# Two changes to the order of VectorE's work in a fused two-layer decoder: paired softmax blocks, and dense steps issued behind the dots

## Chip, core and metric

The kernel runs on one core of a Trainium2 chip. The metric is the device time of one launch in microseconds (us), the lower the better. TensorE is called PE here, VectorE DVE, ScalarE ACT, GpSimd POOL and SyncE SP, as in the profile. Each engine takes its instructions in the order in which they stand in the built program.

## What is computed

Two decoder layers over 512 tokens of width 1024, in float32. Cut to what matters:

```python
for l in range(2):
    m   = x @ w_in[l]                                   # q, k, v, two LRU branches, two gates
    ya  = diff_attention(q, k, v)                       # 8 heads, two causal ALiBi softmax maps each:
                                                        #   (softmax(q1 k1) - lam * softmax(q2 k2)) @ v
    yr  = rg_lru(conv4(xr)) * gelu(gr)
    x   = layer_norm(ALPHA * x + (sig(ga) * (ya @ wa) + sig(gb) * (yr @ wb)) @ w_out)
    # PEER: per token 8 heads x 16 experts of 16384, chosen by two top-16s and a top-16 of their sums
    e, g = route(x)                                     # 128 expert numbers and weights per token
    x   = layer_norm(ALPHA * x + sum_j g[j] * gelu(x . u[e[j]]) * v[e[j]])
```

## The kernel before

The tokens are four blocks of 128 rows (one token per partition). `experts(l, b)` serves one block: for each of its 128 expert places j, POOL gathers one row of 2048 floats (u and v) per token with an indirect DMA (L819, 1 MB in all) into one of 8 buffers `uvt`. DVE then takes the **dot** of u with x (L822), ACT applies gelu (L829), DVE makes the weight `w` (L784), and v is added up in one of two ways: on DVE into `acc` (L790), or by ACT making a diagonal `dg` (L794) and PE two matmuls into `pv` (L796). A buffer is free for a new gather when this is done. Four blocks in two layers make 1024 places, numbered 0 to 1023 below; "dot 450" is the dot of place 450.

Everything else is called **dense**. `mixer` (attention, LRU, merges, output product) handles two blocks at a time and streams its weights as 512 KB pieces through 5 buffers `w` (L253, L275 are its matmuls). `route` (matmuls L656, L663) scores the keys; on DVE `top16` (L716 to L721) and `choose` (L728 to L767) turn the scores into the expert numbers `e` (L761) and weights `g`. `route_late` runs `choose` for the second block of a pair. "Routing" below means L716 to L767.

In the softmax of the attention, `softmax(h, i, b, po, st)` takes one head and one of the two blocks through: scores on PE into the PSUM tile `s2` (one buffer, L386), bias and row maximum on DVE (L390 to L396), two Exp on ACT (L398), a combination on DVE (L402 to L407), transposes on PE through `pt` (one buffer, L412) and the product with v into `po` (L417). The tile `pr` has two buffers; `choose` uses the same two for its one-hot tables `oh` (L753 to L758).

Two things set the order. First `run` records three streams, `gathers()`, `dense()` and `late()`, each with a clock, always going on with the one whose clock is lowest. The clock of `gathers` counts places; `PLAN` gives the dense stages their stretch of places (mixer of layer 0, blocks 2 and 3: places 30 to 222; its routing 222 to 270; its late choice 270 to 370; the same for layer 1: 270 to 470, 470 to 526, 526 to 620, and 526 to 730, 730 to 786, 786 to 880). Within a stage the yielded numbers are shares of its stretch. Second, the framework's scheduler orders the recorded instructions of each engine anew: by recorded place, but an instruction that is ready sooner by the scheduler's own estimate may be put ahead. The class `Load` counts, in recorded order, which of DVE and PE has less to do, and so chooses between L790 and L796.

Of the kernel before, what the change touches and what calls it, by code (L numbers as in the profile page):

```python
# [18 lines left out]
ALU = mybir.AluOpType  # L19
# [3 lines left out]
D = 1024  # L23
# [97 lines left out]
class Decoder:  # L121
# [227 lines left out]
    def attention(self, l, cst, blocks, x, ya, on):  # L349


        nc, t2 = self.nc, self.t2
# [25 lines left out]
        def softmax(h, i, b, po, st):  # L378
# [15 lines left out]
            nm, sm = st[:, i, 0:2], st[:, i, 2:4]  # L394
            nc.vector.tensor_reduce(nm, pr[:, :, :nk], AX.X, ALU.max)
            nc.vector.tensor_scalar(nm, nm, -0.125, None, ALU.mult)  # L396
            for m in range(2):
                nc.scalar.activation(pr[:, m, :nk], pr[:, m, :nk], AF.Exp,  # L398
                                     bias=nm[:, m : m + 1], scale=0.125,
                                     accum_out=sm[:, m : m + 1])  # L400
            yield 2.0
            nc.vector.reciprocal(st[:, i, 4:6], sm)  # L402

            nc.vector.scalar_tensor_tensor(out=st[:, i, 6:7], in0=st[:, i, 5:6],
# [42 lines left out]
        def heads(h):  # L447
            po = self.ps_t.tile([P, 512], F32, name="po", tag="po")
            st = t2.tile([P, 4, 8], F32, name="at_st", tag="at_st")
            for i, b in enumerate(blocks):  # L450
                yield from softmax(h, i, b, po, st)
            nc.scalar.copy(on[:, h, :n], po[:, :n])

        yield from project(0)
# [319 lines left out]
    def experts(self, l, b, G=2):  # L774
# [28 lines left out]
        for j0 in range(0, P, G):  # L803
# [12 lines left out]
            for i in range(G):  # L816
                j = j0 + i
                t = self.gp.tile([P, 2 * D], F32, name="uvt", tag="uv")
                nc.gpsimd.indirect_dma_start(  # L819
                    out=t, out_offset=None, in_=self.uv,  # L820
                    in_offset=bass.IndirectOffsetOnAxis(ap=e[:, j : j + 1], axis=0))
                nc.vector.scalar_tensor_tensor(out=t[:, :D], in0=t[:, :D], scalar=1.0, in1=x,  # L822
                                               op0=ALU.mult, op1=ALU.mult,
                                               accum_out=dots[:, i : i + 1])
                uvs.append(t)
                if i == 0:
                    next(prev, None)
                else:
                    nc.scalar.activation(q, dots, AF.Gelu_apprx_tanh)  # L829
                yield 1  # L830
# [10 lines left out]
    def run(self):  # L841
        nc = self.nc
        self.setup()
        self.cst = [None] * DEPTH
        self.done = set()
        self.load = Load(nc)

        def gathers():
# [35 lines left out]
        while any(live):  # L884
            free = [i for i in range(3) if live[i] and (wants[i] is None or wants[i] in self.done)]
            i = min(free, key=lambda i: (at[i], -i))
            wants[i] = None
            c = next(streams[i], None)
            if c is None:
                live[i] = False  # L890
            elif isinstance(c, tuple):
# [39 lines left out]
```

## Time and profile before

| | |
|---|---|
| median of 3 runs (lowest, highest) | 3445.73 us (3443.23, 3445.84) |
| the profiled execution: its own time | 3443.5 us |
| its span, first to last instruction | 3441.3 us |
| first dot, last gather's landing | about 306 us, about 3422 us |
| busy: PE, DVE, ACT, POOL | 2962.3, 2660.9, 1242.6, 1307.3 us |
| moved by DMA | 1290.5 MB, of which 1073.8 MB by the gathers' queue |
| chain that ended last | PE 44%, DVE 24%, DMA 19% |

A window of the trace gives each engine's busy time in a stretch, the clock granted to PE (1.00 is full), the mean busy share of the 16 DMA engines (it can read a little over 1) and the GB/s that they moved. The windows below are cut at the start of every 32nd dot, so that each holds 32 places. Records of consecutive short instructions overlap; busy time counts the overlap once. A PE matmul of float32 has two records.

### The profile page before, as it was taken

How to read it: one execution, taken by the hardware profiler on the slowest of the kernel's cores; microseconds unless marked ns; L12 is line 12 of the kernel's file. 1: busy time of each engine (PE TensorE's matmuls, PEld its weight loads, DVE VectorE, ACT ScalarE, POOL GpSimd, SP SyncE). 2: the span in 40 equal slices, each digit the busy share in tenths (PEclk: the TensorE clock that was granted, in tenths of full speed). 3: DMA queues.
4: the chain of work that ended last, by engine and by line, in shares of the span. 5: the costliest groups of instructions: out<-in, count | busy, mean ns of one | idle time of the engine just before them, and what ended most of it. 6: DMA issues, size and time to landing. Idle time of an engine off the chain costs nothing.

```text
span 3441.3 us, 38208 instructions
## 1 busy us (share of the span) xinstructions
PE 2962.3 (86%) x11832; PEld 1899.5 (55%) x11832; DVE 2660.9 (77%) x6622; ACT 1242.6 (36%) x2851; POOL 1307.3 (38%) x1033
## 2 busy tenths in 40 slices
PE   8997999999997899999996799999998687656655
PEld 8896666777763466677763366666755232212111
DVE  7765989887689577867699569777679965777776
ACT  7852356652122364633122236644122221111111
POOL 0001334444333434434333433433433344565553
PEclk9998999999999999999997999999999799877677
DMA  5455899999999999999998999999999899999997
GB/s 202 155 174 204 332 408 397 414 418 418 418 398 354 380 392 401 393 417 412 418 389 342 412 393 391 401 413 419 418 412 353 312 405 421 421 422 410 421 422 317
DMA packets 219114, 1290.54 MB, mean 375 GB/s; under 512 B 24593, under 2 KB 37137, under 8 KB 87841
## 3 DMA queue, kind: packets, MB, share of 16 engines
q0 software_dynamic: 147456, 1073.81, 77.0%
q1 hardware_dynamic: 71456, 214.30, 16.4%
q8 instruction: 96, 1.57, 0.2%
q14 instruction: 106, 0.86, 0.1%
HBM read 1285.92 MB, written 2.10 MB: 374 GB/s over the span
## 4 chain that ended last, share of the span: by engine, by line
PE 44%; DVE 24%; DMA 19%; issue 6%; POOL 3%; ACT 3%; POOLq 0%; SPq 0%; DVEq 0%; ACTq 0%
DMA uvt<-uv_dram,e 19%; PE ps_mm L253 18%; PE pv L796 16%; DVE uvt L822 8%; POOL uvt L819 3%; DVE acc L790 3%; PE ps_mm L275 3%; PE ps_ln L313 1%; PE ps_qk L253 1%; DVE oh L756 1%; DVE ef L758 1%; PE s L386 1%; DVE oh L753 1%; PE ps_mm L656 1%; PE po L417 1%
## 5 line engine op out<-in xcount | busy, mean ns | idle before, releaser
L819 POOL DMA_INDIRECT uvt<-uv_dram,e x1024 | 1304.7, 1274 | 2101.5 <-PE pv L796 655.1
L796 PE MATMUL pv<-uvt,dg 128*128 128x512 f32 x2712 | 1417.4, 662 | 379.3 <-ACT dg L794 377.8
L822 DVE SCALAR_TENSOR_TENSOR uvt<-uvt,xn 128x1024 f32<-128x1024 f32 x1024 | 1243.8, 1220 | 248.3 <-DMA uvt<-uv_dram,e 244.4
L796 PEld LDWEIGHTS pv<-uvt,dg 128*128 128x128 f32 x2712 | 527.8, 206 | 1094.7 <-ACT dg L794 604.4
L253 PE MATMUL ps_mm<-room_xT,w 128*128 128x256 f32 x2304 | 538.6, 380 | 0.7 <-ACT room_xT L285 0.7
L829 ACT ACTIVATE q<-dots 128x2 f32<-128x2 f32 x512 | 104.1, 203 | 1132.3 <-DVE uvt L822 1117.4
L253 PEld LDWEIGHTS ps_mm<-room_xT,w 128*128 128x128 f32 x2304 | 430.4, 190 | 108.8 <-issue 53.9
L790 DVE SCALAR_TENSOR_TENSOR acc<-uvt,w,acc 128x1024 f32<-128x1024 f32 x346 | 443.6, 1282 | 7.9
L794 ACT ACTIVATE dg<-ident,w 128x128 f32<-128x128 f32 x678 | 257.4, 398 | 290.3 <-DVE w L784 171.1
L784 DVE TENSOR_TENSOR w<-q,g 128x2 f32<-128x2 f32 x512 | 80.7, 158 | 208.9 <-ACT q L829 203.9
L656 PE MATMUL ps_mm<-room_xT,w 128*128 128x256 f32 (+1 forms) x1056 | 241.5, 377 | 0.0
L656 PEld LDWEIGHTS ps_mm<-room_xT,w 128*128 128x128 f32 x1056 | 194.7, 194 | 42.7 <-issue 19.9
L829 ACT ACT_TABLE_LOAD x115 | 147.5, 1283 | 19.6 <-DVE uvt L822 17.0
L238 DVE TENSOR_TENSOR wsp<-raw,wsp 128x1024 fp32r<-128x1024 f32 x80 | 97.1, 1222 | 27.0 <-ACT wsp L237 24.8
L275 PEld LDWEIGHTS ps_mm<-w,room_xT 128*128 128x128 f32 x768 | 90.8, 192 | 8.5 <-issue 7.1
L275 PEld LDWEIGHTS ps_mm<-w,room_m 128*128 128x128 f32 x768 | 89.2, 192 | 9.2 <-issue 8.4
L275 PE MATMUL ps_mm<-w,room_xT 128*128 128x128 f32 x768 | 92.6, 275 | 0.0
L253 PE MATMUL ps_mm<-room_yr,w 128*128 128x256 f32 x384 | 90.1, 380 | 0.0
L253 PE MATMUL ps_mm<-room_ya,w 128*128 128x256 f32 x384 | 89.5, 379 | 0.0
L275 PE MATMUL ps_mm<-w,room_m 128*128 128x128 f32 x768 | 89.3, 275 | 0.0
L237 ACT CAST wsp<-raw 128x1024 fp32r<-128x1024 f32 x80 | 82.7, 1052 | 14.8 <-PE ps_mm L253 7.8
L822 DVE DVE_READ_ACCUMULATOR uvt<-uvt,xn 128x1 f32 x1024 | 84.1, 82 | 0.0
(196 smaller groups left out, 2980.7 us busy)
## 6 DMA issues: line engine op xcount, KB each, us to landing
w<-wpk_dram SPq DMA_DIRECT2D x304, 512.0 KB
raw<-wpk_dram SPq DMA_DIRECT2D x80, 512.0 KB
uvt<-uv_dram,e POOLq DMA_INDIRECT x1024
gw<-gpk_dram SPq DMA_DIRECT2D x32, 128.0 KB
sk<-spk_dram SPq DMA_DIRECT2D x64, 64.0 KB
xn<-x_dram SPq DMA_DIRECT2D x4, 512.0 KB
out_dram<-xn SPq DMA_DIRECT2D x8, 256.0 KB
lq<-lqk_dram SPq DMA_DIRECT2D x2, 128.0 KB
```

Source lines behind the costliest of these rows:

```text
L237: self.nc.scalar.copy(hi, raw)
L238: self.nc.vector.tensor_tensor(lo, raw, hi.bitcast(F32), ALU.subtract)
L253: self.nc.tensor.matmul(ps[:, :n], w, x, start=i == 0, stop=i == len(steps) - 1)
L275: self.nc.tensor.matmul(out[:, i], x(slice(i * P, (i + 1) * P)), w, start=j == 0, stop=j == len(steps) - 1)
L656: nc.tensor.matmul(pq[:, :n], w[:, kc, :], self.acts_x.plain[:, kc, t0 : t0 + n], start=kc == 0, stop=kc == KC - 1)
L784: nc.vector.tensor_tensor(w, q, g[:, j0 : j0 + G], ALU.mult)
L790: nc.vector.scalar_tensor_tensor(out=acc, in0=t[:, D:], scalar=w[:, i : i + 1], in1=acc, op0=ALU.mult, op1=ALU.add)
L794: nc.scalar.activation(dg, self.ident, AF.Copy, scale=w[:, i : i + 1])
L796: nc.tensor.matmul(pv[:, half], dg, t[:, D + half * 512 : D + (half + 1) * 512], start=not began[0], stop=j == P - 2)
L819: nc.gpsimd.indirect_dma_start(out=t, out_offset=None, in_=self.uv, in_offset=bass.IndirectOffsetOnAxis(ap=e[:, j : j + 1], axis=0))
L822: nc.vector.scalar_tensor_tensor(out=t[:, :D], in0=t[:, :D], scalar=1.0, in1=x, op0=ALU.mult, op1=ALU.mult, accum_out=dots[:, i : i + 1])
L829: nc.scalar.activation(q, dots, AF.Gelu_apprx_tanh)
```

## The change

Three edits. In `softmax` the step that ended after the Exp is cut in two, with a yield after the row maximum. `heads` takes both blocks of a head through `softmax` in step (`zip`) where it took one block after the other. And each dot is remembered in `self.dot`; whatever `dense()` and `late()` then record on DVE gets an order edge to the last recorded dot: it has to stand behind it in DVE's queue, with no wait for it to finish.

```diff
@@ softmax
             nc.vector.tensor_scalar(nm, nm, -0.125, None, ALU.mult)
+            yield 1.0
             for m in range(2):
                 nc.scalar.activation(pr[:, m, :nk], pr[:, m, :nk], AF.Exp,
                                      bias=nm[:, m : m + 1], scale=0.125,
                                      accum_out=sm[:, m : m + 1])
-            yield 2.0
+            yield 1.0
@@ heads
-            for i, b in enumerate(blocks):
-                yield from softmax(h, i, b, po, st)
+
+            for costs in zip(*(softmax(h, i, b, po, st) for i, b in enumerate(blocks))):
+                yield sum(costs)
@@ experts
-                nc.vector.scalar_tensor_tensor(out=t[:, :D], in0=t[:, :D], scalar=1.0, in1=x,
-                                               op0=ALU.mult, op1=ALU.mult,
-                                               accum_out=dots[:, i : i + 1])
+                self.dot = nc.vector.scalar_tensor_tensor(
+                    out=t[:, :D], in0=t[:, :D], scalar=1.0, in1=x, op0=ALU.mult, op1=ALU.mult,
+                    accum_out=dots[:, i : i + 1]).ins
@@ run
-            c = next(streams[i], None)
+            if i and self.dot is not None:
+
+                with self.tc.issue_after(self.dot):
+                    c = next(streams[i], None)
+            else:
+                c = next(streams[i], None)
```

After the edits line numbers from 397 on are one higher, from the end of `heads` on two higher (L824 is the dot, L786 `w`, L792 `acc`, L798 `pv`).

What the built programs hold: 4960 DVE instructions before and 4957 after, 2645 and 2620 on ACT (300 and 272 of them table loads), 346 and 343 times L790. Counted between dots in DVE's order, the routing instructions:

| places | 192-223 | 224-255 | 256-287 | 416-447 | 448-479 | 480-511 | 512-543 | 672-703 | 704-735 | 736-767 | 768-799 | 800-863 |
|---|---|---|---|---|---|---|---|---|---|---|---|---|
| before | 153 | 171 | 31 | 73 | 226 | 25 | 32 | 55 | 222 | 155 | 0 | 0 |
| after | 0 | 217 | 105 | 0 | 30 | 190 | 102 | 0 | 20 | 190 | 114 | 108 |

The accumulations L790 stand where they stood: 14, 3, 2, 16, 13, 0, 3, 16, 13, 2, 1 in these windows (the last apart). Of the dense DVE instructions recorded between dots 448 and 511 the mean one stood 41 dots ahead of its recorded place before, between dots 64 and 127 0.6 dots ahead, between dots 0 and 63 2.1 dots behind; now none stands ahead.

DVE, layer 1's routing of blocks 0 and 1. Each L822 or L824 row is a dot; the first row of both pieces is dot 455. Before:

```order
L822 SCALAR_TENSOR_TENSOR uvt_12912,dots_12910<-uvt_12912,xn1_4375 128x1024
L790 SCALAR_TENSOR_TENSOR acc_11704<-uvt_12865,w_12915,acc_11704 128x1024
L758 TENSOR_REDUCE ef_13550<-oh_13562 128x16
L822 SCALAR_TENSOR_TENSOR uvt_12922,dots_12910<-uvt_12922,xn1_4375 128x1024
L756 TENSOR_TENSOR oh_13581<-oh_13581,ca_13532 128x864
L784 TENSOR_TENSOR w_12931<-q_12911,g3_115 128x2
L716 MAX sv_13611<-sc_13635 128x8
L790 SCALAR_TENSOR_TENSOR acc_11704<-uvt_12922,w_12931,acc_11704 128x1024
L822 SCALAR_TENSOR_TENSOR uvt_12928,dots_12926<-uvt_12928,xn1_4375 128x1024
L758 TENSOR_REDUCE ef_13550<-oh_13581 128x16
L718 MAX_INDEX si_13612<-sv_13611,sc_13635 128x8
L761 CAST e0_108<-ef_13550 128x32
```

Now, from dot 455 on:

```order
L824 SCALAR_TENSOR_TENSOR uvt_12918,dots_12916<-uvt_12918,xn1_4375 128x1024
L824 SCALAR_TENSOR_TENSOR uvt_12928,dots_12916<-uvt_12928,xn1_4375 128x1024
L786 TENSOR_TENSOR w_12937<-q_12917,g3_115 128x2
L792 SCALAR_TENSOR_TENSOR acc_11712<-uvt_12928,w_12937,acc_11712 128x1024
L824 SCALAR_TENSOR_TENSOR uvt_12934,dots_12932<-uvt_12934,xn1_4375 128x1024
L824 SCALAR_TENSOR_TENSOR uvt_12944,dots_12932<-uvt_12944,xn1_4375 128x1024
L786 TENSOR_TENSOR w_12953<-q_12933,g3_115 128x2
L792 SCALAR_TENSOR_TENSOR acc_11712<-uvt_12944,w_12953,acc_11712 128x1024
```

The routing (L716, L718, L753 to L761) has left this place. DVE thirty dots on, from dot 487, before:

```order
L822 SCALAR_TENSOR_TENSOR uvt_13372,dots_13370<-uvt_13372,xn1_4375 128x1024
L822 SCALAR_TENSOR_TENSOR uvt_13400,dots_13370<-uvt_13400,xn1_4375 128x1024
L784 TENSOR_TENSOR w_13434<-q_13371,g3_115 128x2
L822 SCALAR_TENSOR_TENSOR uvt_13431,dots_13429<-uvt_13431,xn1_4375 128x1024
L822 SCALAR_TENSOR_TENSOR uvt_13444,dots_13429<-uvt_13444,xn1_4375 128x1024
L784 TENSOR_TENSOR w_13475<-q_13430,g3_115 128x2
```

Now, from dot 487:

```order
L824 SCALAR_TENSOR_TENSOR uvt_13378,dots_13376<-uvt_13378,xn1_4375 128x1024
L718 MAX sv_13318<-sc_13353 128x8 x2
L720 MAX_INDEX si_13319<-sv_13318,sc_13353 128x8 x2
L723 MATCH_REPLACE sc_13353<-sv_13318,sc_13353 128x128 x2
L718 MAX sv_13318<-sc_13353 128x8 x2
L720 MAX_INDEX si_13319<-sv_13318,sc_13353 128x8 x2
L824 SCALAR_TENSOR_TENSOR uvt_13406,dots_13376<-uvt_13406,xn1_4375 128x1024
L718 MAX top0_12897<-sc_13355 128x8 x2
```

Here it stands now, in the stretch that `PLAN` gives it. PE, one head of the second mixer (places 32 to 64), before:

```order
L386 MATMUL s2_5027<-kT0_104,qT_4802 128x256
L386 MATMUL s2_5027<-kT1_4376,qT_4802 128x128
L386 MATMUL s2_5027<-kT0_104,qT_4802 128x256
L386 MATMUL s2_5027<-kT1_4376,qT_4802 128x128
L253 MATMUL ps_mm_5042<-room_xT_4378,w_5043 128x256 x8
L796 MATMUL pv_3552<-uvt_5009,dg_5062 128x512 x2
L489 MATMUL pg_5075<-xc_5068,gw_4986 128x256
L386 MATMUL s2_5183<-kT0_104,qT_4802 128x256
L386 MATMUL s2_5183<-kT1_4376,qT_4802 128x256
L489 MATMUL pg_5078<-xc_5068,gw_4986 128x256
L253 MATMUL ps_mm_5094<-room_xT_4378,w_5095 128x256
L412 MATMUL pt_5088<-ident_88,pr_5032 128x128 x3
```

Now:

```order
L386 MATMUL s2_5027<-kT0_104,qT_4803 128x256
L386 MATMUL s2_5027<-kT1_4376,qT_4803 128x128
L386 MATMUL s2_5027<-kT0_104,qT_4803 128x256
L386 MATMUL s2_5027<-kT1_4376,qT_4803 128x128
L253 MATMUL ps_mm_5049<-room_xT_4378,w_5050 128x256 x4
L386 MATMUL s2_5036<-kT0_104,qT_4803 128x256
L386 MATMUL s2_5036<-kT1_4376,qT_4803 128x256
L386 MATMUL s2_5036<-kT0_104,qT_4803 128x256
L386 MATMUL s2_5036<-kT1_4376,qT_4803 128x256
L253 MATMUL ps_mm_5049<-room_xT_4378,w_5050 128x256 x4
```

The scores of the head's second block follow four projection matmuls behind the first block's; its first transposes (L413, not in the piece) stand 30 matmuls behind them.

## Rows read from the trace of the kernel before

**Rows 1.** Page, 40 equal slices of 86 us: DMA share in tenths, GB/s

```profile
DMA  5455899999999999999998999999999899999997
GB/s 202 155 174 204 332 408 397 414 418 418 418 398 354 380 392 401 393 417 412 418 389 342 412 393 391 401 413 419 418 412 353 312 405 421 421 422 410 421 422 317
```

**Rows 2.** Windows: stretch, length, busy us (records) of PE PEld DVE ACT POOL, PEclk, DMA, GB/s

```profile
436.00:537.60 101.60, 99.23 (x409) 67.04 (x410) 90.18 (x249) 56.14 (x119) 41.47 (x32) 1.00 0.99 394
736.90:840.90 104.00, 102.31 (x453) 76.27 (x452) 85.70 (x161) 38.39 (x82) 46.88 (x33) 1.00 1.02 418
950.00:1058.60 108.60, 97.03 (x376) 65.02 (x376) 97.48 (x332) 27.48 (x84) 42.93 (x32) 0.97 1.00 399
1058.60:1152.80 94.20, 70.60 (x162) 32.03 (x163) 83.47 (x307) 25.43 (x66) 38.49 (x32) 0.91 0.90 341
1152.80:1256.90 104.10, 99.39 (x347) 60.07 (x346) 63.35 (x163) 45.13 (x97) 36.66 (x32) 0.95 0.99 397
1665.10:1776.60 111.50, 102.06 (x500) 73.35 (x499) 88.67 (x263) 24.40 (x71) 38.98 (x32) 0.95 1.00 408
1776.60:1885.00 108.40, 77.52 (x229) 42.23 (x227) 108.40 (x416) 26.69 (x70) 42.07 (x32) 0.86 0.92 354
1885.00:1962.90 77.90, 61.65 (x130) 24.90 (x131) 45.89 (x89) 15.08 (x49) 32.30 (x32) 0.96 0.99 402
1962.90:2067.00 104.10, 99.05 (x358) 60.67 (x356) 68.39 (x164) 43.13 (x96) 36.71 (x32) 0.95 0.99 393
2471.00:2579.80 108.80, 100.56 (x480) 69.29 (x479) 82.57 (x236) 21.26 (x60) 39.31 (x33) 0.94 1.01 414
2579.80:2688.20 108.40, 84.99 (x282) 50.34 (x281) 108.37 (x404) 26.59 (x77) 40.85 (x32) 0.89 0.92 347
2688.20:2780.50 92.30, 63.74 (x121) 25.23 (x120) 84.89 (x258) 28.30 (x61) 38.44 (x32) 0.87 0.88 330
2943.00:3022.50 79.50, 47.30 (x77) 16.01 (x76) 57.60 (x95) 10.66 (x35) 45.34 (x32) 0.82 1.01 421
```

**Rows 3.** Waits in 1776.6 to 1885.0: who waited for whom, us, times, longest

```profile
POOL uvt L819 <- PE pv L796: 18.7, 7, 6.6
POOL uvt L819 <- DVE acc L790: 11.3, 3, 7.5
POOL uvt L819 <- DVE top L716: 9.6, 4, 4.3
```

**Rows 4.** DVE groups, 1776.6 to 1885.0: line, op, shapes, count | busy, mean ns | idle before

```profile
L822 DVE SCALAR_TENSOR_TENSOR uvt<-uvt,xn 128x1024 f32<-128x1024 f32 x33 | 39.9, 1210 | 0.0
L790 DVE SCALAR_TENSOR_TENSOR acc<-uvt,w,acc 128x1024 f32<-128x1024 f32 x13 | 16.5, 1272 | 0.0
L784 DVE TENSOR_TENSOR w<-q,g 128x2 f32<-128x2 f32 x16 | 2.4, 148 | 0.0
```

**Rows 5.** DMA issues on the page: size of one weight piece

```profile
w<-wpk_dram SPq DMA_DIRECT2D x304, 512.0 KB
```

**Rows 6.** POOL groups, in 1776.6 to 1885.0, then in 2862.0 to 3022.5

```profile
L819 POOL DMA_INDIRECT uvt<-uv_dram,e x32 | 42.1, 1315 | 68.8 <-PE pv L796 18.7 <-DVE acc L790 11.3 <-DVE top L716 9.6
...
L819 POOL DMA_INDIRECT uvt<-uv_dram,e x64 | 83.2, 1299 | 76.7 <-PE pv L796 47.6 <-DVE acc L790 17.2 <-issue 5.9
```

**Rows 7.** ACT groups of the whole span: the table loads ahead of gelu and Exp

```profile
L829 ACT ACT_TABLE_LOAD x115 | 147.5, 1283 | 19.6 <-DVE uvt L822 17.0 <-DVE at_st L402 0.6
...
L398 ACT ACT_TABLE_LOAD x64 | 82.1, 1283 | 1.1
```

**Rows 8.** DVE's waits over the whole span

```profile
DVE uvt L822 <- DMA uvt<-uv_dram,e: 244.4, 244, 3.2
...
DVE at_st L402 <- ACT pr L398: 16.5, 23, 2.5
...
DVE oh L753 <- PE po L417: 1.0, 3, 0.6
```

**Rows 9.** Window before the first gather, columns as in group 2

```profile
0.00:260.00 260.00, 243.62 (x1929) 231.88 (x1930) 183.94 (x420) 191.96 (x364) 2.57 (x9) 1.00 0.52 177
```

More of the change, by code (lines that the diff above doesn't have):

```diff
@@ L845, in run @@
         self.done = set()
+        self.dot = None
         self.load = Load(nc)
```

## Prediction, made before the changed kernel was run

> **What bounds the kernel now.** I read the page's slices first. From the fifth slice on the DMA share is at 8 to 9 tenths and the rate mostly between 390 and 422 GB/s, but it falls to 354 and 380, 389 and 342, 353 and 312 [rows 1]: three dips, one per routing after the first. So the gathers and the weights fill the DMA engines, and what can be won is in the dips. Then I cut the trace at every 32nd dot, because the change is about where work stands between dots. An undisturbed window without weights takes 79.5 us at 421 GB/s; a mixer window with its weights takes 104.0 us at 418, with PE busy for 102.3 of it [rows 2]. Both run as fast as the DMA engines go. In the dips DVE is full: 108.40 us of 108.40 in places 448 to 479, 108.37 of 108.40 in 704 to 735, 84.89 of 92.30 in 736 to 767, 97.48 of 108.60 in 192 to 223, while PE sinks to 64 to 85 us and its granted clock to 0.86 to 0.91 [rows 2]. POOL shows how this reaches the DMA: it waits to issue the next gather for `acc` and even for a MAX8 of the routing, which are no producers of its buffer but the instructions behind which the releasing one had queued on DVE [rows 3]. The cause is in the order, not in the amount of work: DVE's queue holds the routing some 40 dots ahead of its recorded place, packed into one window (226 routing instructions in places 448 to 479, 25 in the next one), while `Load` had given that window 13 accumulations on DVE as if the routing were not there. The window behind it then has too little for DVE: 45.89 us of 77.90 [rows 2].
>
> **What a dip costs.** At 418 GB/s the bytes of a window would take (rate/418) of its time. The excess by [rows 2], in order of place: dip one (192 to 255) 4.9 + 17.4 = 22.3 us; dip two (416 to 511) 2.7 + 16.6 + 3.0 = 22.3; dip three (672 to 767) 1.0 + 18.4 + 19.4 = 38.8. In all 83.4 us. That is the pool from which the tie can draw.
>
> **The tie (issue behind the dots).** It adds no instruction and no semaphore; it moves the routing back to the stretch that `PLAN` gives it. Price of the routing per instruction: in 1776.6 to 1885.0, 108.4 us busy, less 32 dots of 1.210 (38.7), 13 accumulations (16.5) and `w` (2.4) [rows 4], leaves 50.8 us for 226 instructions, 0.225 us each. In 2688.2 to 2780.5, 84.9 less 38.7, 2.4 and two accumulations of 1.272 leaves 41.3 for 155, 0.266 each (more of them one-hot passes). With the counts of the order after, DVE has to do:
>
> - places 224 to 255: 38.7 + 2.4 + 3 x 1.272 + 217 x 0.225 to 0.266 = 94 to 103 us;
> - 480 to 511: 41.1 + 190 x the same = 84 to 92 us;
> - 736 to 767: 41.1 + 2 x 1.272 + 190 x the same = 86 to 94 us;
> - the windows that the routing leaves (192, 448 and 704 on): under 75 us, since at most 30 routing instructions stay.
>
> DMA needs 79.5 us for 32 gathers plus 1.25 us for each weight piece of 512 KB at 418 GB/s [rows 2, 5]. The score matmuls in PE's order after (79, 50 and 73, eight to a piece) put 9.9, 6.2 and 9.1 pieces into the first three: 91.9, 87.3 and 90.9 us. So DVE and DMA are about level there: DVE is over by 2 to 11 us in the first, by -3 to 5 and -5 to 3 in the others. Nowhere is there a second window like 448 to 479, where DVE's 108.4 us stood against 91.8 us of bytes (108.4 x 354/418).
>
> What stays: a window in which all three engines are this busy has not run at 418 in the trace but at 393 to 397 (places 256 to 287 and 512 to 543), a loss of 5.2 and 6.2 us [rows 2]. I take 8 us for the first heavy window (it is also over by some 6 at mid-range), 5 and 6 for the other two, 3 for each of the three that were emptied, and 2 for place 768 on, which now gets 114 routing instructions but has only 79.5 us of gathers to meet: 8 + 5 + 6 + 9 + 2 = 30 us. The tie gains 83.4 - 30 = **53 us**. Bounds: 83 if nothing stays, 23 if twice as much stays.
>
> Nothing waits in exchange by the order: the expert numbers of the block that starts at place 256 stand behind dot 234 (was 211), those for 512 behind 484 (448), for 768 behind 744 (708). With 8 buffers POOL wants them 8 places early, so 14, 20 and 16 places are left, at 2.5 us a place 35 us or more. What is late next is DMA itself.
>
> **The paired softmax.** No operation is added. Table loads fall from 300 to 272: 28 x 1.283 us [rows 7] = 36 us of ACT. ACT is busy for 56 of 101.6 us in an attention window [rows 2], and DVE's waits on Exp add up to 16.5 us in the whole span [rows 8]: I take 0, with 16 as the most to be won. In the first 260 us, which the tie doesn't reach, PE is busy for 243.6 [rows 9]; with some 11 us of that idle time at the start, 5 us is the most to be won. To be lost: the pair holds both `pr` buffers at once and the late choice's one-hot tables want the same two. DVE waits for one of them 1.0 us in all, 3 times [rows 8]. Taking 0.3 us for each of the 48 one-hot chains of the three late choices that fall beside a mixer gives 16 us; I take 0, as DVE and PE have other work queued there.
>
> **Sum.** 3443.5 us (the profiled execution's own time: the span of 3441.3 and 2.2 around it) - 53 = 3390.5. The median of the runs, 3445.73, is 2.2 us above that execution, so I say **3392 us**, 1.6% less.
>
> **Rivals.** (a) *Slower: dots block the dense steps.* DVE takes its queue in order, and dots wait for gathers: 244 times, 1.0 us in the mean [rows 8]. A softmax step behind a waiting dot passes that on to PE, whose transposes and products stand in one queue with `pv`, and `pv` frees the gathers' buffers. The 24 heads of the three mixers beside gathers have 4 steps each: 96 waits of 1.0 us would be 96 us, 3443.5 - 53 + 96 = 3486. It decides from 0.55 us a step. Against it: in places 0 to 127 the old order already has the dense steps about where they were recorded (2.1 dots behind and 0.6 ahead in the mean of its halves), and PE is busy for 99.2 of 101.6 us in places 32 to 63, at 394 GB/s [rows 2]. The Trainium skill ("Perfetto Trace Analysis", Per-instruction lifecycle) says that PE can pull weight loads ahead while "ACT/DVE/GPSIMD are strict FIFO": by that rule nothing on DVE can pass a waiting dot, which is this rival; no row here shows an instruction passing another.
>
> (b) *No change: POOL was held by the port, not by the buffers.* If DVE's running instructions themselves lengthened POOL's gather issue, the same DVE work later would cost the same: 3443.5. Then an issue should take longer in a dip than in a calm stretch; it takes 1315 ns against 1299 [rows 6]. The Trainium skill ("SBUF — State Buffer", Two separate sides) has such a rule: VectorE and GpSimd share a port pair, and descriptors made on GpSimd starve while VectorE holds it. The rows give it 0.016 us x 32, half a us per dip.
>
> (c) *Less: the heavy windows become the new dips.* If DVE's waits on PE and ACT inside the score chain make each heavy window 10 us longer than taken (PE's own routing matmuls now stand among the dots there), the gain is 53 - 30 = 23: 3420.
>
> (d) *More: the paired softmax also lifts the attention stretches to 418 GB/s.* Six slices of the page run at 391 to 401 there (392, 401, 393 and 393, 391, 401) [rows 1] and lose 28 us by the same reckoning: 3443.5 - 83 - 28 = 3332.
>
> That the tie does nothing is excluded by the counts of the order.
>
> **How the numbers follow.** Chances: the forecast (30 to 80 us gained) 0.60, (c) 0.16, (d) 0.08, (b) or a balance of gains and losses 0.05, (a) 0.11. A measurement of this kernel can tell about 0.2%, 7 us, from no change. Faster is 0.60 + 0.16 + 0.08 = 0.84, same 0.05, slower 0.11. The range goes from 3350 (the tie's bound of 83 with some of the softmax's) to 3432, through (c) as far as a gain of 12 us; it leaves out (d), (a) and (b), with the far ends some 0.2.
>
> **What would show it.** Right: no window of 32 dots with DVE busy over 98% of it; the dips at places 448 and 704 gone, those windows at 90 to 96 us and over 400 GB/s; places 480 to 511 longer than 77.9 us (about 92); PE's clock over 0.9 in all of them; DMA share 0.97 or more from 436 us on. Wrong: DVE idle before dots while PE waits on DVE in the mixers (a); POOL waiting on the routing's L761 behind dots 234, 484 or 744; or the three heavy windows over 105 us (c).

## The result, and the profile after

The changed kernel takes 3409.28 us (median of 4 runs, 3407.21 to 3417.96) against 3445.78 for the kernel before (3443.23 to 3446.22): a ratio of 0.990, 95% interval 0.9882 to 0.9919. That is 36.5 us less. The forecast was 3392 us, 53 us less, with a range of 3350 to 3432. Sign and range hold; the gain is two thirds of the one forecast.

The profiled execution took 3407.21 us, its span 3405.4. First the page, with the lines that answer to [rows 1] and [rows 7]: busy time by engine, then DMA share and GB/s in 40 slices of 85 us, the shares of the chain that ended last, and the table loads ahead of gelu.

```profile
PE 2953.0 (87%) x11844; PEld 1904.5 (56%) x11844; DVE 2654.6 (78%) x6619; ACT 1208.6 (35%) x2826; POOL 1331.9 (39%) x1033
...
DMA  5455899999999999999999999999999989999997
GB/s 193 165 173 200 311 409 411 396 418 418 419 408 404 356 411 390 416 418 403 418 408 412 387 408 395 391 393 413 416 418 411 385 353 422 421 422 414 422 422 311
...
PE 50%; DMA 21%; DVE 16%; ACT 6%; issue 5%; POOL 3%; SPq 0%; POOLq 0%; DVEq 0%; ACTq 0%
...
L831 ACT ACT_TABLE_LOAD x99 | 127.0, 1283 | 10.0 <-DVE uvt L824 5.1
```

The dips are narrower: 354 and 380, 389 and 342, 353 and 312 GB/s [rows 1] have become 356, 387 and 385 with 353. No engine's amount of work has moved much: DVE was busy for 2660.9 us and is for 2654.6. On the chain DVE went from 24% to 16% and PE from 44% to 50%.

Now the windows of 32 places, as in [rows 2] (columns: stretch, length, busy us and records of PE, PEld, DVE, ACT, POOL, PEclk, DMA share, GB/s). Of the kernel after, in order: places 192, 224, 256, 448, 480, 512, 704, 736 and 768 on.

```profile
945.30:1041.30 96.00, 79.55 (x312) 48.75 (x311) 64.84 (x123) 20.79 (x60) 41.53 (x32) 0.89 1.00 410
1041.30:1145.00 103.70, 94.56 (x316) 57.15 (x314) 96.35 (x391) 25.82 (x81) 38.61 (x32) 0.96 1.00 397
1145.00:1241.40 96.40, 86.54 (x278) 49.88 (x279) 83.05 (x291) 47.28 (x100) 34.82 (x31) 0.95 0.93 373
...
1749.10:1842.80 93.70, 80.62 (x264) 47.33 (x262) 68.99 (x174) 18.48 (x63) 41.00 (x32) 0.90 1.00 408
1842.80:1938.90 96.10, 88.88 (x291) 51.72 (x292) 85.59 (x320) 30.34 (x86) 37.46 (x31) 1.00 1.00 401
1938.90:2031.40 92.50, 86.39 (x278) 49.23 (x277) 80.16 (x250) 41.65 (x87) 39.26 (x33) 0.94 0.97 392
...
2545.10:2638.90 93.80, 75.62 (x216) 39.48 (x215) 66.79 (x142) 21.62 (x63) 41.54 (x31) 0.80 1.01 412
2638.90:2738.50 99.60, 93.45 (x325) 57.22 (x323) 89.78 (x357) 26.68 (x83) 36.15 (x32) 1.00 0.96 383
2738.50:2826.00 87.50, 66.83 (x135) 26.14 (x134) 72.98 (x237) 24.35 (x60) 41.65 (x34) 0.90 0.92 364
```

Places 448 and 704 on, DVE's full windows of 108.4 us, now take 93.7 and 93.8 at 408 and 412 GB/s. In exchange 224 on went from 94.2 to 103.7 and 480 on from 77.9 to 96.1.

One reckoning makes windows comparable, the prediction's own: what a window loses is its length times (1 - rate/418). All losses together account for the change of the span to within 1 us in the change and the tie alone (5 us in the pairing alone), since the bytes are the same. By group, in us (dips: places 192 to 287, 416 to 543, 672 to 799; mixers: the other places from 32 to 671; the first 32 places apart; the span is that of the profiled execution):

| | first 32 | dips | mixers | rest | span |
|---|---|---|---|---|---|
| before | 21.1 | 94.9 | 29.6 | -1.9 | 3441.3 |
| after | 25.3 | 50.3 | 35.1 | -2.5 | 3405.4 |
| tie alone | 22.6 | 55.6 | 20.7 | -0.3 | 3396.7 |
| pairing alone | 24.1 | 102.8 | 43.1 | -2.5 | 3469.7 |

So the change wins 44.6 us in the dips and loses 5.5 in the mixers and 4.2 in the first stretch: 35 of the span's 35.9 us. Each row is one execution. The change with four weight buffers for five, a kernel of the same time (below), reads 22.9, 46.4, 36.5 and -1.9, so a difference of some 4 us in one group says little.

### The profile page after: what moved, and what is told of

Same layout as the page of the kernel before. It is cut to its first block, busy times and chain, and to the rows that moved or that the text cites. A ratio compares the mean times of both kernels' runs of the same rounds, so it can differ in the third digit from the quotient of the medians.

```text
span 3405.4 us, 38230 instructions
## 1 busy us (share of the span) xinstructions
PE 2953.0 (87%) x11844; PEld 1904.5 (56%) x11844; DVE 2654.6 (78%) x6619; ACT 1208.6 (35%) x2826; POOL 1331.9 (39%) x1033
## 4 chain that ended last, share of the span: by engine, by line
PE 50%; DMA 21%; DVE 16%; ACT 6%; issue 5%; POOL 3%; SPq 0%; POOLq 0%; DVEq 0%; ACTq 0%
DMA uvt<-uv_dram,e 21%; PE pv L798 19%; PE ps_mm L253 16%; DVE uvt L824 5%; PE ps_mm L658 5%; PE ps_mm L275 4%; POOL uvt L821 3%; DVE acc L792 2%; PE ps_ln L313 1%; PE ps_sc L665 1%; PE s L386 1%; DVE oh L755 1%; DVE ef L760 1%; PE po L418 1%; PE ps_qk L253 1%
## 5 line engine op out<-in xcount | busy, mean ns | idle before, releaser
L821 POOL DMA_INDIRECT uvt<-uv_dram,e x1024 | 1329.3, 1298 | 2041.4 <-PE pv L798 778.9
L798 PE MATMUL pv<-uvt,dg 128*128 128x512 f32 x2724 | 1411.2, 655 | 321.4 <-ACT dg L796 320.2
L824 DVE SCALAR_TENSOR_TENSOR uvt<-uvt,xn 128x1024 f32<-128x1024 f32 x1024 | 1243.7, 1220 | 266.4 <-DMA uvt<-uv_dram,e 260.6
L798 PEld LDWEIGHTS pv<-uvt,dg 128*128 128x128 f32 x2724 | 530.4, 205 | 986.0 <-ACT dg L796 506.4
L253 PEld LDWEIGHTS ps_mm<-room_xT,w 128*128 128x128 f32 x2304 | 438.5, 192 | 121.2 <-issue 54.2
L792 DVE SCALAR_TENSOR_TENSOR acc<-uvt,w,acc 128x1024 f32<-128x1024 f32 x343 | 440.3, 1284 | 10.6 <-ACT acc L813 0.2
L786 DVE TENSOR_TENSOR w<-q,g 128x2 f32<-128x2 f32 x512 | 80.6, 157 | 245.1 <-ACT q L831 235.9
L658 PEld LDWEIGHTS ps_mm<-room_xT,w 128*128 128x128 f32 x1056 | 196.1, 195 | 44.2 <-issue 21.9
L275 PEld LDWEIGHTS ps_mm<-w,room_m 128*128 128x128 f32 x768 | 92.6, 197 | 19.1 <-issue 10.4
L534 ACT ACTIVATE mth<-ps_mm 128x256 f32<-128x256 f32 x64 | 24.5, 383 | 201.3 <-PE ps_mm L253 201.2
L253 PEld LDWEIGHTS ps_mm<-room_ya,w 128*128 128x128 f32 x384 | 71.4, 190 | 34.9 <-ACT mth L534 16.6
```

The source lines that it names most:

```text
L253: self.nc.tensor.matmul(ps[:, :n], w, x, start=i == 0, stop=i == len(steps) - 1)
L275: self.nc.tensor.matmul(out[:, i], x(slice(i * P, (i + 1) * P)), w, start=j == 0, stop=j == len(steps) - 1)
L658: nc.tensor.matmul(pq[:, :n], w[:, kc, :], self.acts_x.plain[:, kc, t0 : t0 + n], start=kc == 0, stop=kc == KC - 1)
L786: nc.vector.tensor_tensor(w, q, g[:, j0 : j0 + G], ALU.mult)
L792: nc.vector.scalar_tensor_tensor(out=acc, in0=t[:, D:], scalar=w[:, i : i + 1], in1=acc, op0=ALU.mult, op1=ALU.add)
L798: nc.tensor.matmul(pv[:, half], dg, t[:, D + half * 512 : D + (half + 1) * 512], start=not began[0], stop=j == P - 2)
```

## Experiments

The theory to be tested: the routing stood too dense between the dots, DVE's queue could not serve the dots in time, so the buffers came free late; the tie cures this, and the pairing is worth nothing. Against it stand a cost of the tie (dots that block dense steps), a cost of the pairing, and PE or the accumulations as the true limit of the crowded windows. Every kernel was compared with the kernel before on its own chip; that one stood at 3445.7 to 3448.3 us each time.

**The two halves apart.** The tie alone, that is the change with the pairing taken out:

```diff
-            yield 1.0
             for m in range(2):                  # the Exp
...
-            yield 1.0
+            yield 2.0
...
-            for costs in zip(*(softmax(h, i, b, po, st) for i, b in enumerate(blocks))):
-                yield sum(costs)
+            for i, b in enumerate(blocks):
+                yield from softmax(h, i, b, po, st)
```

> Only the order edge behind the dots; the softmax goes one block after the other as before. If the tie carries the whole gain (my term of 0 for the paired softmax): 3405 to 3414 us, as the changed kernel's 3409, with places 448 to 479 at 94 us or less. If the paired softmax carries a part of it: over 3418 us.

Measured: 3396.16 us (5 runs, 3391.92 to 3399.64), ratio 0.9844 (0.983 to 0.9857). That is 52 us less than before by the medians, 49 to 56 over its runs; its profiled execution, whose span of 3396.7 us the tables use, is one of its slower ones. And the pairing alone, the change with the edge to the dot left out:

> Only the paired softmax, no order edge. If it is worth nothing: 3440 to 3450 us, the three dips still there (places 448 to 479 at about 108 us with DVE full). If it is a part of the gain: 3425 to 3438 us. If it costs time, for instance through the two pr buffers that the one-hot tables want too: over 3452 us, and then the tie alone must be faster than the change.

Measured: 3471.5 us (3467.99 to 3475.07), ratio 1.0065 (1.0051 to 1.0079): 23 us slower than before. Beside the tie the pairing costs 13 us by the medians (3409.3 against 3396.2), or 16 when each kernel is taken from the kernel before on its own chip (36.5 us less against 52.1). In the pairing alone the third dip grew. These are its places 736 on, columns as above:

```profile
2706.30:2808.50 102.20, 67.61 (x124) 26.65 (x124) 100.60 (x355) 30.97 (x66) 41.50 (x31) 0.85 0.84 305
```

Against [rows 2] the window is 9.9 us longer, with DVE full and 305 GB/s. In its order 218 routing instructions stand there, 155 before: without the tie, the scheduler moves the routing when the softmax is rewritten. The table above shows the rest of the loss in the mixers (29.6 to 43.1).

**Whether the accumulations fill the dips.** The kernel before, with those of the crowded windows put on PE:

```diff
                 vector = self.load.dve + 1.22 <= self.load.pe + 1.72
+                n = (4 * l + b) * P + j
+                if 192 <= n < 256 or 448 <= n < 480 or 704 <= n < 768:
+                    vector = False
```

> The kernel before, with the routing as early as it was, but in places 192 to 255, 448 to 479 and 704 to 767 every accumulation goes to PE: 16, 13 and 14 fewer on DVE, 1.28 us each, 55 us in all. If the dips are DVE's fullness in these windows: 30 to 50 us off, 3396 to 3416 us, places 448 to 479 at 92 to 96 us. If the dips come from the routing instructions themselves holding up POOL's gathers (rival b): 3438 to 3448 us, as those stand where they stood.

Measured: 3451.18 us, ratio 1.0007 (0.9998 to 1.0016): nothing. DVE was relieved all the same, as places 448 on show; below the window stand all waits of DVE in it (who waited for whom, us, times, longest).

```profile
1785.40:1893.20 107.80, 91.36 (x282) 50.58 (x281) 96.29 (x407) 30.70 (x85) 38.31 (x32) 0.97 0.94 360
```

```profile
DVE sv L716 <- ACT sc L670: 10.4, 3, 4.7
DVE w L784 <- ACT q L832: 0.8, 3, 0.3
```

Busy time fell from 108.40 us [rows 2] to 96.29, but now DVE stands for 10.4 us before the first MAX8 of a `top16`, which waits for scores that ACT has not copied yet. 96.3 + 10.4 + 0.8 is 107.5 of 107.8 us: the queue is as full as before, with a wait in the place of the work. Both expectations failed here, and the run corrects the reading of the dips: DVE's queue is held by what waits in it as well as by its work. Why the scores come late is not settled. The routing may stand too early, or the accumulations that are now on PE may stand ahead of the score matmuls: ACT's wait for these doubled (the same places before, then in this run), and POOL's for `pv` rose from 18.7 us [rows 3] to 44.6.

```profile
ACT sc L670 <- PE ps_sc L663: 6.3, 6, 2.3
...
ACT sc L670 <- PE ps_sc L663: 12.5, 6, 3.7
```

So moving accumulations from DVE to PE does not help while the order stays; what less work in all would do was not tried.

**How dense the routing may stand.** Three kernels with the tie alone and other stretches in `PLAN`. In the first the routing gets 32, 40 and 40 places for 48, 56 and 56; in the second the mixers end 14 to 16 places earlier and it gets 62, 72 and 72:

```diff
-    (0, [2, 3], 30, 222, 270, 370),
-    (1, [0, 1], 270, 470, 526, 620),
-    (1, [2, 3], 526, 730, 786, 880),
+    (0, [2, 3], 30, 222, 254, 370),   # first     # second:    30, 208, 270, 370
+    (1, [0, 1], 270, 470, 510, 620),              #            270, 454, 526, 620
+    (1, [2, 3], 526, 730, 770, 880),              #            526, 714, 786, 880
```

> The tie alone (e1, 3396 us) with the three later routings squeezed by the plan: places 222 to 254, 470 to 510 and 730 to 770. Places 224 to 255, 480 to 511 and 736 to 767 then hold 305, 245 and 265 routing instructions in DVE's order (217, 190, 190 in e1). If the routing's density between the dots makes a dip, also with the tie: DVE needs 113 to 125, 96 to 106 and 102 to 112 us there (103.7, 96.6 and 100.0 us in e1), the windows behind them get some back, 3400 to 3425 us. If these windows are as long as they are for DMA's or PE's sake: 3390 to 3400 us.

> The tie alone with the three routings spread: places 208 to 270, 454 to 526 and 714 to 786. The same three windows hold 152, 148 and 148 routing instructions, the ones before them 70, 94 and 74. If density makes the loss: 93 to 96 us in each of the three, 3380 to 3390 us, faster than the tie alone. If the mixers, which get 14 to 16 places less, lose as much because PE is full there: 3392 to 3402 us.

Measured: 3424.07 us (ratio 0.9935, 0.9918 to 0.9951) and 3391.27 us (0.9848, 0.9831 to 0.9864). The windows from place 224 on, of the tie alone, of the squeezed and of the spread routing, with 217, 305 and 152 routing instructions in the order, one line from each kernel:

```profile
1041.20:1144.90 103.70, 94.62 (x316) 57.02 (x314) 96.30 (x390) 25.73 (x81) 38.89 (x32) 0.94 1.00 399
```

```profile
1045.90:1161.60 115.70, 98.86 (x323) 58.01 (x322) 113.56 (x505) 33.83 (x92) 34.13 (x32) 0.96 0.95 364
```

```profile
1055.00:1147.30 92.30, 84.31 (x262) 46.20 (x260) 80.02 (x308) 27.56 (x78) 37.11 (x34) 1.00 1.00 404
```

103.7, 115.7 and 92.3 us: the window's length follows the routing in it, and so it does at 480 (96.6, 103.5, 95.1) and 736 (100.1, 112.3, 89.6). A longer window also moves more bytes, so not all of it is lost. By the reckoning above the three kernels lose 4.7, 14.9 and 3.1 us at 224, 4.2, 15.6 and 3.2 at 480, 8.9, 19.1 and 4.1 at 736, and 55.6, 82.1 and 44.1 us in all dips. So squeezing the routing brings a good part of the dips back, also with the tie, and spreading it wins less than the lengths say. The window of the squeezed kernel at 224 is DVE's alone: 113.56 us busy and one wait group left, which is the whole rest of the 115.7 us:

```profile
DVE uvt L823 <- DMA uvt<-uv_dram,e: 2.1, 2, 2.0
```

The spread does not get all of this as time: its mixers have 14 to 16 places less, and places 64 to 95 went from 98.5 to 107.8 us. The third kernel keeps the mixer of layer 0 as it was and spreads the routing of layer 1 alone:

> The tie without the pairing, with the mixers of layer 1 ending 16 places earlier (454 and 714 for 470 and 730), so that each routing of layer 1 has 72 places for its 56; layer 0 keeps its stretch. If the routing's density sets the heavy windows and squeezing a mixer costs only what e6_spread showed in the windows concerned (layer 0 lost 4.3 us there, the two of layer 1 gained 1.7 and 6.3), the time is 3383 to 3391 us, less than both e1_tie_only (3396) and e6_spread (3391), with 148 routing instructions in places 480 to 511 and 736 to 767 at 89 to 95 us. If the windows' gains and losses don't add up (a gain in one is given back in the next, since the DMA engines have the same bytes to move), it is 3391 to 3397 us.

Measured: 3396.9 us (4 runs, 3389.88 to 3399.61), ratio 0.986 (0.9844 to 0.9877). Its profiled execution is the fastest of the four; there the heavy windows of layer 1 take 93.6 and 91.4 us and the span is 3388.1, as adding up the windows had it. The other three are at 3396 to 3400, like the tie alone. So the gains of single windows are not shown to add up. The spread has the lowest median of all kernels here, 3391.27 us, but by the ratios to the kernel before on the same chip (0.9844, 0.9848, 0.986) the tie alone, the spread and this one can't be told apart. All three are faster than the change, whose interval begins at 0.9882.

The opposite, a routing that ends 12 places later (222 to 282, 470 to 538, 730 to 798, the next mixers from 282 and 538 on):

> The tie alone with the three routings spread toward later places (222 to 282, 470 to 538, 730 to 798; the mixers behind begin 12 places later), so that no mixer is squeezed as in e6. 168, 148 and 158 routing instructions in the three heavy windows (217, 190, 190 in e1), 152, 152 and 140 in the ones behind them. By density: 94 to 98 us in the heavy windows, 95 to 98 behind the first two, 3383 to 3393 us. If the gain of the heavy windows is lost behind them, where the late choice and the next mixer begin: 3393 to 3402 us.

Measured: 3407.84 us, ratio 0.9883 (0.9866 to 0.9899), 12 us slower than the tie alone and outside both expectations. The heavy windows got shorter (98.2, 95.9 and 95.7 us) with 168, 148 and 158 routing instructions, but they lose no less in sum: 5.2, 6.7 and 8.0 us for 4.7, 4.2 and 8.9. More is lost in places 192 (6.2 us for 2.0), 320 (6.4 for 1.2) and 704 on (5.9 for 1.6). By the groups of the table the dips lose 64.4 us for 55.6, the mixers 20.7 as with the tie alone. A mixer that begins later may explain places 320 and 704 on, but not 192 on, where the plan is that of the tie alone. So the density of the routing is not the whole account; what this kernel loses by stays open.

**Whether PE sets the heavy windows.** PE is busy for 94.6 of 103.7 us there. The tie alone, with half of PE's expert work left out in places 224 to 255, 480 to 511 and 736 to 767 and DVE's order kept:

```diff
-                    for half in range(2):
+                    n = (4 * l + b) * P + j
+                    k = 2
+                    if j < P - 2 and (224 <= n < 256 or 480 <= n < 512 or 736 <= n < 768):
+                        k = 1
+                        self.load.pe += 0.009 + 512 / 596
+                    for half in range(k):
```

> The tie alone, with the second of the two pv matmuls left out in places 224 to 255, 480 to 511 and 736 to 767 (29, 32 and 30 places that accumulate on PE): some 26 us less on PE in each, DVE's order as in e1. If the rest of the loss in these windows (103.7, 96.6, 100.0 us in e1) is PE, on which the score matmuls and nearly all accumulations now stand: each shorter by 5 to 12 us, 3370 to 3385 us. If DVE's routing alone sets them: within 2 us of e1 in each, 3390 to 3400 us.

Measured: 3400.53 us (2 runs), ratio 0.9865 (0.9845 to 0.9884), not faster than the tie alone. Places 224 on:

```profile
1042.50:1143.60 101.10, 77.36 (x264) 48.88 (x262) 96.30 (x390) 27.72 (x85) 36.62 (x32) 0.90 1.02 412
```

PE lost 17 us of work and the window 2.6 us. DVE's 96.30 us are untouched, and so nearly is the window's length. By the reckoning it loses 1.5 us for 4.7, but the windows at 480 and 736 lose 6.1 and 7.8 for 4.2 and 8.9, so the three together lose 15.4 for 17.8. PE is not what sets them.

**Whether dots block the mixers' steps.** Rival (a) asked for a kernel in which only the routing is tied, not the mixers' DVE steps (without the pairing):

```diff
-            if i and self.dot is not None:
+            if i and self.dot is not None and (i == 2 or self.routing):
```

`self.routing` is set while `dense()` records a `route` and cleared for a `mixer`.

> The tie for the routing and the late choice alone; the mixers' DVE steps are free as before, the softmax goes one block after the other. If the gain is the routing's place: 3390 to 3402 us, as e1. If tying the mixers' steps costs time because they wait behind dots (rival a): 3375 to 3389 us. If the mixers gain by it too: over 3403 us.

Measured: 3416.45 us, ratio 0.9912 (0.9896 to 0.9929). The routing's tie gives 30 us, and the mixers' tie another 20, where rival (a) wanted a loss. By the reckoning the mixers lose 30.1 us, as before the change (29.6), where the tie alone loses 20.7; the dips lose 62.9 for 55.6, most of the difference in places 256 on (14.9 for 9.9). Why the mixers gain by being tied was not tried.

**What the pairing costs.** The two windows that grew most against the tie alone are 288 on (105.4 us for 98.8) and 576 on (107.6 for 100.1), where a late choice runs beside a mixer. Two kernels: the change with 4 weight buffers for 5, which makes room, and that one with a third buffer for `pr` and `oh`:

```diff
-        self.wp = pool("weights", 5)
+        self.wp = pool("weights", 4)          # both kernels
...
-            pr = t2.tile([P, 2, 512], F32, name="pr", tag="pr")
+            pr = t2.tile([P, 2, 512], F32, name="pr", tag="pr", bufs=3)     # the second; oh likewise
```

> The changed kernel (both edits, 3409 us) with 4 weight buffers in place of 5, which frees 4 KB per partition: the base for the next kernel. 3405 to 3440 us.

> The same with a third buffer for pr in the freed room. If the 13 us that the paired softmax costs beside the tie (3409 against 3396) come from the pair holding both pr buffers, which the late choice's one-hot tables also want: 8 to 14 us less than with 4 weight buffers and two pr, with places 288 to 351 and 576 to 607 shorter. If they come from something else (order on PE, the one s2 buffer, bigger steps on DVE): within 4 us of it.

Measured: 3409.47 us (3404.62 to 3411.16), the same as the change, and 3404.53 us (3403.9 to 3406.32), ratio 0.988. Places 576 on of the change, then of the third buffer:

```profile
2131.60:2239.20 107.60, 102.56 (x440) 69.07 (x439) 89.92 (x205) 60.63 (x127) 40.41 (x34) 0.98 0.95 381
```

```profile
2132.80:2233.90 101.10, 99.92 (x439) 67.68 (x438) 85.58 (x200) 62.40 (x129) 41.82 (x33) 1.00 1.00 402
```

With a buffer more the window is nearly as short as without the pairing. POOL's waits in the change's window (who waited for whom, us, times, longest):

```profile
POOL uvt L821 <- PE pv L798: 24.8, 11, 4.5
POOL uvt L821 <- DVE sm_st L767: 16.4, 2, 12.0
POOL uvt L821 <- DVE acc L792: 11.2, 3, 5.7
```

The longest wait of the third row, 5.7 us up to 2149.5, is for an accumulation that frees a buffer and stands behind steps of the late choice. In DVE's order of time (start, us, line, shape, idle before):

```profile
2141.95 1.06 DVE L755 TENSOR_TENSOR oh<-iota,pf 128x864 f32<-128x864 f32 x1 [0.38 <-PE po L418]
2142.93 1.22 DVE L824 SCALAR_TENSOR_TENSOR uvt<-uvt,xn 128x1024 f32<-128x1024 f32 x1
...
2144.07 1.05 DVE L758 TENSOR_TENSOR oh<-oh,ca 128x864 f32<-128x864 f32 x1
2145.04 1.05 DVE L755 TENSOR_TENSOR oh<-iota,pf 128x864 f32<-128x864 f32 x1
2146.01 1.05 DVE L760 TENSOR_REDUCE ef<-oh 128x16 f32<-128x864 f32 x1
2146.97 1.05 DVE L758 TENSOR_TENSOR oh<-oh,ca 128x864 f32<-128x864 f32 x1
2147.94 1.28 DVE L792 SCALAR_TENSOR_TENSOR acc<-uvt,w,acc 128x1024 f32<-128x1024 f32 x1
2149.13 1.05 DVE L760 TENSOR_REDUCE ef<-oh 128x16 f32<-128x864 f32 x1
2150.10 1.22 DVE L824 SCALAR_TENSOR_TENSOR uvt<-uvt,xn 128x1024 f32<-128x1024 f32 x1
```

The chain waits for `po`, since a pair holds both `pr` buffers until its product with v; then two one-hot chains come at once and stand 6 us between two dots. The 12.0 us of the second row are another wait, up to 2210.5: two such chains stand there as well, from 2194.7 to 2200.7, but behind them also steps of the mixer, so the chains are only a part of it. With the third buffer POOL has no wait on L767 in this window.

The third buffer shortens the two windows by 14 us and the time by some 5 only, between its two expectations; the intervals of the two kernels (0.9875 to 0.9908 and 0.9863 to 0.9896) overlap. The rates tell a part of why. At 288 the change already ran at 409 GB/s; the shorter window has 397, so it moves fewer bytes and wins nothing. At 576 the rate rose from 381 to 402, a loss of 9.5 us that became 3.9. By the groups of the table the mixers now lose 25.0 us, for 36.5 with four weight buffers and 35.1 in the change, near the 20.7 of the tie alone: what the pairing loses in the mixers goes for the most part with the shared buffers. But the dips lose 52.9 us for 46.4 (50.3 in the change), 5.6 of it in places 704 on, where both others lose 1.3. Why the dips take a part back was not tried and stays open.

**Whether the routing should also stand behind `w` and `acc`.** The change, with the dense steps tied to the last dot, `w` or accumulation, whichever was recorded last:

```diff
-            nc.vector.tensor_tensor(w, q, g[:, j0 : j0 + G], ALU.mult)
+            self.dot = nc.vector.tensor_tensor(w, q, g[:, j0 : j0 + G], ALU.mult).ins
...
-                    nc.vector.scalar_tensor_tensor(out=acc, in0=t[:, D:], scalar=w[:, i : i + 1],
-                                                   in1=acc, op0=ALU.mult, op1=ALU.add)
+                    self.dot = nc.vector.scalar_tensor_tensor(
+                        out=acc, in0=t[:, D:], scalar=w[:, i : i + 1], in1=acc, op0=ALU.mult,
+                        op1=ALU.add).ins
```

> The changed kernel, with the dense steps tied behind the last recorded w or accumulation too, not behind the last dot alone. If what the heavy windows still lose comes from routing that stands between a dot and the steps that free its buffer (POOL waits up to 12.7 us behind such an instruction): 8 to 20 us less than the change, 3389 to 3401 us, places 768 to 799 at 82 us instead of 87.5. If DVE then waits for gelu at w with the routing queued behind, or if these windows are simply full: 3405 to 3420 us.

Measured: 3411.66 us (3404.92 to 3414.09), ratio 0.9885 (0.9869 to 0.9901), no gain over the change. Places 768 on stay at 88.2 us for 87.5, so what is lost there is not shown to be the order between dot and `w`.

## Why the forecast came out as it did

**The pool (83.4 us) and what the tie takes of it: right.** The windows that made up the 83.4 us now lose, in order of place, 1.8 and 5.2, then 0, 2.2 and 3.9, then 0, 1.3 and 8.3: 22.7 us. The prediction left 28 there (8, 5 and 6 for the heavy windows, 3 for each emptied one). Gain: 60.7 us, taken: 55.

**DVE's work by window: right.** Forecast 94 to 103, 84 to 92 and 86 to 94 us; 96.35, 85.59 and 89.78 came. The price of 0.225 to 0.266 us a routing instruction is near, a little high: from the tie alone to the squeezed kernel 88 instructions added 17.3 us of DVE to places 224 on (0.196 each) and 75 added 18.1 to 736 on (0.242).

**"DVE and DMA are about level there": only half.** DVE's queue is what sets the length. In places 224 on it waited, in all, for this:

```profile
DVE w L786 <- ACT q L831: 5.0, 6, 2.0
DVE sm_st L767 <- ACT ef L766: 1.4, 1, 1.4
DVE uvt L824 <- DMA uvt<-uv_dram,e: 0.7, 1, 0.7
```

96.35 + 5.0 + 1.4 + 0.7 is 103.5 of 103.7 us, and only 0.7 of it is for gathers. The sum of DVE's busy time lacked the waits of `w` for gelu, which hold the queue. Over the span they rose from 203.9 us in 291 waits to 235.9 in 292. That they rose because the routing that used to fill these gaps now stands elsewhere is my reading, not shown. The same count explains why places 480 and 736 on took 96.1 and 99.6 us for 85.59 and 89.78 of work (waits of 10.1 and 9.6 us).

The bytes were mis-sized too: at 418 GB/s those that the three windows moved take 98.5, 92.2 and 91.3 us, where 91.9, 87.3 and 90.9 were forecast. So a window that DVE makes longer is not all lost. The terms of 8, 5 and 6 us came as 5.2, 3.9 and 8.3, near in sum, but their reason was a wrong reading: a window in which all three engines are busy has run at 418, places 128 on, with PE at 102.31 and DVE at 85.70 of 104.00 us [rows 2]. Another reading that the rows do not bear is that PE sinks in all the dips: in places 192 on it was busy for 97.03 us at a clock of 0.97 [rows 2].

**The windows behind the heavy ones: the term that was mis-sized.** Places 256 and 512 on were left out, and place 768 on had 2 us. Before, these three lost 11.4 us; now 10.4, 5.8 and 11.3, in all 27.5. That is 16 us for 2, and it comes from the tie, since the tie alone loses 9.9, 7.8 and 13.2 there. By the counts of the order 105, 102 and 114 routing instructions now stand there. The step that failed is that place 768 on "has only 79.5 us of gathers to meet": DVE was busy for 72.98 us there, less than that, and the window took 87.5. For this window the loss goes with the routing over the runs: 0.0 us with none (before), 8.3 with 50 (squeezed), 13.2 with 108 (tie alone) and 12.2 with 140 (late), counted by start in the trace. For places 512 on it does not go so plainly (6.2 us with 33 before, 3.6 with 88 in the spread kernel, 7.8 with 108 in the tie alone). POOL's waits in places 768 on, the longest groups:

```profile
POOL uvt L821 <- PE pv L798: 21.7, 15, 5.4
POOL uvt L821 <- DVE top L720: 12.7, 1, 12.7
```

The 12.7 us are one wait, from 2743.8 to 2756.5. In DVE's queue there stand routing instructions between the dots, and also the layer norm of the block that ends at place 767, so the routing is not alone in it; how the 11.3 us of loss divide is not shown.

**The paired softmax taken as 0: wrong by 13 us**, inside the bound of 16 as it was stated. The step that failed is "DVE and PE have other work queued there". The bound itself was miscounted: the eight choices have 64 one-hot chains in all (64 times L753 in the trace), so the three late ones have 24 and not 48, and 24 times 0.3 us is 7 us, less than the pairing costs. (48 times 0.3 is 14.4; the 16 come with a third of 1.0 us each.) The mechanism named there, the `pr` buffers shared with `oh`, is a true one: DVE's waits for a buffer rose from 1.0 us [rows 8] to 7.0, and the third buffer wins some 5 us. The gains are there too. DVE's waits on Exp fell from 16.5 us [rows 8] to 4.2 (12.4 with the tie alone), and the table loads from 300 to 272 (289 with the tie alone). What they are worth by themselves was not tried; the pairing as a whole is a loss.

```profile
DVE oh L755 <- PE po L418: 7.0, 7, 2.7
DVE at_st L403 <- ACT pr L399: 4.2, 7, 1.7
```

So the sum is: -60.7 in the old dips, +16.1 behind them, +5.5 in the mixers and +4.2 at the start, -35 us. The tie alone brought 52 us by the medians where 53 were forecast, but not by the forecast's terms. In its profiled execution (44.6 us less) it took 58.6 from the old dips for 55, lost 19.5 behind them for 2, and won 8.9 in the mixers, on which nothing had been counted. That the medians meet the 53 is partly luck.

**The rivals.** (a) is refuted: tying the mixers' steps gains 20 us. Dots waited for gathers 257 times and 260.6 us in all, against 244 and 244.4 [rows 8]; but the dense steps behind a dot don't make PE late enough to show: the tie alone loses less in the mixers than the kernel before (20.7 for 29.6). (b) is refuted, for the same DVE work placed later costs 45 us less in the dips. POOL's issue took 1206 ns in DVE's busiest window and 1449 in one that ran at 421 GB/s (places 224 on, then 832 on; columns: count, busy, mean ns, idle before):

```profile
L821 POOL DMA_INDIRECT uvt<-uv_dram,e x32 | 38.6, 1206 | 65.5 <-PE pv L798 25.6 <-DVE acc L792 9.7 <-DVE ef L760 9.0
```

```profile
L821 POOL DMA_INDIRECT uvt<-uv_dram,e x32 | 46.4, 1449 | 33.3 <-PE pv L798 14.6 <-DVE acc L792 11.8 <-issue 3.4
```

The Trainium skill ("SBUF — State Buffer", SBUF: two separate sides, the "DVE blocks DMA" trap) has descriptors starved while VectorE runs an instruction in a 2-port mode and so holds the shared port; with this kernel's instructions the trace shows no sign of it, the window with DVE busy for 93% having shorter issues than places 864 on with 76% (1518 ns). (c) did not happen as told, no heavy window being over 105 us, but a relative of it did: what was lost stands one window later. (d) fell: the attention stretches did not rise, the mixers lose 35.1 us for 29.6.

**The signs named in advance.** No window has DVE over 98% busy (93% at most): right. The emptied windows at 93.7 and 93.8 us, over 400 GB/s: right. Places 480 on at 96.1 for some 92: right in kind. PE's clock over 0.9 in all of them: wrong, it is 0.89 and 0.90 in places 192 and 448 on and 0.80 in 704 on, at 410, 408 and 412 GB/s; a window bound by DMA leaves PE idle, and its clock is no measure of a dip. DMA share of 0.97 or more: wrong, it is 0.93 and 0.92 in places 256 and 768 on, which is the term above, and 0.95 and 0.96 in 576 and 736 on.

## What to carry to other kernels

Where one engine's queue feeds a stream of transfers, add up per stretch how long the queue is held, work and the waits of what stands in it; if the two fill the stretch and it hardly waits for the transfers, look at the order of that queue first; moving work from it to another engine may only turn work into waiting. Compare stretches by what they lose against the full rate, not by their length. Tie side work to the place at which it was planned before tuning how much of it there is, and look at the stretch behind the one that was cured, where the rest of it will stand. Test edits of one change apart: here one gave 52 us and the other took 13 to 16 of it back.

## What of the hardware was not expected

The length of a gather's issue on POOL is not constant. In the mean over 32 places of the changed kernel it is 1131 ns in places 736 on, 1206 in 224 on, 1449 in 832 on and 1518 in 864 on, where no routing stands and the rate is 422 GB/s; over the span 1298. It does not follow DVE's load: in the kernel before it was 1009 ns in places 480 on, with DVE busy for 45.89 of 77.90 us [rows 2]. What sets it was not tried. And PE's granted clock, a mean of its two levels, may be 0.80 in a stretch that runs at 412 GB/s (places 704 on, PE busy for 75.6 of 93.8 us), while it is 1.00 in one at 383 GB/s (736 on, PE busy for 93.5 of 99.6). Here it went with PE's idle time and told nothing of whether the kernel lost there.
